# Splitting fp32 weights with two GpSimd transfers instead of ScalarE and VectorE

## The chip, the cores and the metric

The kernel runs on one core of a Trainium2 chip, as one program of some 18,000 instructions. The metric is the device time of one execution in microseconds. A core has TensorE (PE in the profile; PEld is its weight load), VectorE (DVE), ScalarE (ACT), GpSimd (POOL) and SyncE (SP). Each engine works through its own queue in order; semaphores tie them together. DMAs are issued by SyncE, ScalarE or GpSimd and carried by 16 DMA engines.

## The reference

Two transformer blocks in fp32 on x of 512 x 1024 (d_model 1024, one batch, depth 1):

```python
def first_block(x, ...):
    x = x + 0.5 * swiglu_ffn(rmsnorm(x, ffn1_norm), ffn1_w_gate, ffn1_w_up, ffn1_w_down)   # d_ff 2816
    x = x + hybrid_mixer(rmsnorm(x, mix_norm), w_in, ..., w_out)   # 8 heads of chunked attention + pooling
    x = x + 0.5 * swiglu_ffn(rmsnorm(x, ffn2_norm), ffn2_w_gate, ffn2_w_up, ffn2_w_down)
    return rmsnorm(x, final_norm)

def second_block(x, ...):
    proj = rmsnorm(x, norm_mix_pre) @ w_in
    ...                                   # 4 heads of differential attention, 4 heads of mLSTM
    x = x + rmsnorm(concat(o_diff, o_mlstm) @ w_out, norm_mix_post)
    u = square(relu(rmsnorm(x, norm_mlp_pre) @ w_up))              # d_ff 4096
    return x + rmsnorm(u @ w_down, norm_mlp_post)
```

All weight matrices are fp32, 136 MB together, and each is used once.

## The kernel before, in words

Every product of activations and weights is made of three TensorE products of rounded numbers. An fp32 operand is split into a rounded part (type fp32r) and a remainder (also fp32r); hi x hi, hi x lo and lo x hi are added up in one PSUM bank (`mm3`). The activations' parts are xh and xl (or tiles of the arenas, which the profile calls a1f, a1r, a2f, a2r: f holds fp32, r holds fp32r). The weights' parts are whi and wlo.

The weights are cut into 256 tiles of 128 x 1024 numbers or a little less, listed by `plan` in the order in which TensorE needs them. Most are 8 blocks of 128 rows x 128 columns, so that each partition gets 8 rows of 512 bytes; some (the values' projections, the last MLP's down projection) are 2 blocks x 512 columns, with rows of 2 KB. One tile feeds 24 matmuls of 512 columns. A tile goes through three steps: SyncE loads it into one of three raw buffers (wraw), ScalarE copies it with rounding into one of four whi buffers, and VectorE subtracts whi from wraw into one of four wlo buffers (`split`, called from `w_pump`). `W` hands TensorE's code the tile that is due and lets `w_pump` run two tiles ahead of it; at four places the code asks for four tiles at once.

The code is only noted down at first. Each call becomes an `Op` with its reads, writes and an assumed duration, and `issue` sets the order of each engine's queue by repeated forward and backward sweeps over the graph of dependencies. It runs twice, once for the first block's feed-forward part and mixer (arena a1), once for the rest (a2). A DMA that GpSimd issues is booked there as 1000 ns of GpSimd, one that SyncE issues as 60 ns, and all transfers share one modelled bus. So the order of all queues changes with every edit.

The stages, in time: first feed-forward block (to 377 us), first mixer with attention and pooling (to 560), second feed-forward block (to 925), second block's attention and mLSTM (to about 1195), last MLP. The last MLP's up projections take the 128-column tiles, its down projections the 512-column ones.

Of the kernel before, what the change touches and what calls it, by code (L numbers as in the profile page):

```python
# [9 lines left out]
F32 = mybir.dt.float32  # L10
F32R = mybir.dt.float32r
I32 = mybir.dt.int32
AF = mybir.ActivationFunctionType
ALU = mybir.AluOpType

P = 128
# [4 lines left out]
KD = 8  # L21
EPS = 1e-6
NEG = -1e30
W_BUFS = 4
R_BUFS = 3
SPLIT_AHEAD = 2
ARENA = (5500, 16050)
ARENA2 = (10450, 11050)

# [35 lines left out]
class Program:  # L65
# [84 lines left out]
    def note(self, eng, fn, a, k):  # L150
        outs = list(a[:1]) + [k[n] for n in ("out", "accum_out") if k.get(n) is not None]
        ins = [x for x in a[1:] if self.is_ap(x)]
        ins += [x for n, x in k.items() if n not in ("out", "accum_out") and self.is_ap(x)]
        op = self.add(eng.name, getattr(eng.queue, fn), a, k, self.cost(eng.name, fn, outs, ins, k))
        if "dma" in fn:
            op.dma = max(math.prod(outs[0].shape) / 90.0, 300.0)
            op.lag = 1900.0 + op.dma
        w, r = self.boxes(outs), self.boxes(ins)
        op.opens = eng.name == "PE" and k.get("start", True)
        if fn == "matmul" and not op.opens:  # L160
            r = r + w
        if k.get("func") in (AF.Ln, AF.Exp, AF.Silu, AF.Tanh):
            self.edge(self.load, op)
            self.users.append(op)
        for bs, wr in ((r, False), (w, True)):
            for b in bs:
                for c in self.cells(b):
                    for b2, o2, w2 in self.seen.get(c, ()):
                        if o2 is not op and (wr or w2 or c[0].startswith('bank')) and self.meet(b, b2, op, o2):
                            self.edge(o2, op, w2 and not wr)  # L170
        for b in w:
            for c in self.cells(b):
                self.seen[c] = [x for x in self.seen.get(c, ()) if not self.covers(b, x[0])]
        for bs, wr in ((r, False), (w, True)):
            for b in bs:
                for c in self.cells(b):
                    self.seen.setdefault(c, []).append((b, op, wr))
# [137 lines left out]
class Kern:  # L315
# [114 lines left out]

    def w_init(self, pool):
        self.L = self.plan()
        self.raw = [pool.tile([P, 1024], F32, name=f"wraw{i}") for i in range(R_BUFS)]
        self.wh = [pool.tile([P, 1024], F32R, name=f"whi{i}") for i in range(W_BUFS)]
        self.wl = [pool.tile([P, 1024], F32R, name=f"wlo{i}") for i in range(W_BUFS)]
        self.w_dma = self.w_split = self.w_cur = 0

    def w_view(self, t, i):
        _, _, nk, nc_ = self.L[i]
        return t[:, :nk * nc_].rearrange("p (k c) -> p k c", k=nk)  # L440

    def w_load(self, upto):
        while self.w_dma < min(upto, len(self.L)):
            i = self.w_dma
            self.sp.dma_start(self.w_view(self.raw[i % R_BUFS], i), self.L[i][1])
            self.w_dma += 1

    def w_pump(self, upto):
        while self.w_split < min(upto + 1, len(self.L)):
            i = self.w_split  # L450
            self.w_load(i + R_BUFS)
            m = self.L[i][2] * self.L[i][3]
            step = m // 2 if i < 2 else m
            for c in range(0, m, step):
                c = slice(c, c + step)
                self.split(self.wh[i % W_BUFS][:, c], self.wl[i % W_BUFS][:, c], self.raw[i % R_BUFS][:, c])
            self.w_split += 1
            self.w_load(self.w_split + R_BUFS)

    def W(self, key, ahead=SPLIT_AHEAD):  # L460
        i = self.w_cur
        assert self.L[i][0] == key, (self.L[i][0], key)
        self.w_pump(i + ahead)
        self.w_cur += 1
        return self.w_view(self.wh[i % W_BUFS], i), self.w_view(self.wl[i % W_BUFS], i)

# [83 lines left out]
    def setup(self):  # L550
        tc, I, ctx = self.tc, self.I, self.ctx
        cp = ctx.enter_context(tc.tile_pool(name="cp", bufs=1))
        pp = ctx.enter_context(tc.tile_pool(name="pp", bufs=1, space=bass.MemoryType.PSUM))
        self.B = [pp.tile([P, 512], F32, name=f"bank{i}") for i in range(8)]
        self.mmb = Rot(self.B)
        dp = ctx.enter_context(tc.tile_pool(name="dp", bufs=1, space=bass.MemoryType.DRAM))
        self.tape = dp.tile([8, 16, 384], F32, name="tape")

        T = lambda name, shape, dt=F32: cp.tile(shape, dt, name=name)
        self.w_init(cp)  # L560
        self.X, self.XT = T("X", [P, KD, S]), T("XT", [P, NT, D])
        self.xh, self.xl = T("xh", [P, KD, S], F32R), T("xl", [P, KD, S], F32R)
        self.xs = [(self.xh[:, m, :], self.xl[:, m, :]) for m in range(KD)]
        self.ident, self.onesr = T("ident", [P, P]), T("onesr", [P, P], F32R)
        self.hm2 = T("hm2", [P, 2])
        self.rows1, self.rows, self.cols = T("rows1", [8, P]), T("rows", [NROW, P]), T("cols", [P, 8 + NROW])
        self.rcol = T("rcol", [P, NT])
        self.cv, self.ct, self.cr = (T(n, [P, 16]) for n in ("cv", "ct", "cr"))
        self.gfp = T("gfp", [P, KD])
        self.rsb, self.acc = T("rsb", [P, S]), T("acc", [P, S])  # L570
        self.sqh, self.sql = T("sqh", [P, S], F32R), T("sql", [P, S], F32R)
        self.sq = Rot([T(f"sq{i}", [P, S]) for i in range(2)])

        def load_x(m):
            self.sp.dma_start(self.XT[:, :, m * P:(m + 1) * P],
                              I["x"][0][:, m * P:(m + 1) * P].rearrange("(t p) c -> p t c", p=P))
        self.ac.dma_start(self.rows1, I["ffn1_norm"][0].rearrange("(r c) -> r c", c=P))
        self.po.memset(self.ident, 1.0)
        for s in (1, -1):
            self.po.affine_select(out=self.ident, in_=self.ident, pattern=[[s, P]], base=0, channel_multiplier=-s,  # L580
                                  compare_op=ALU.is_ge, fill=0.0)
        for half in range(2):
            for m in range(4 * half, 4 * half + 4):
                load_x(m)
                if m == 4 * half:
                    for i in range(2):
                        k = slice(m, m + 4)
                        self.sp.dma_start(self.w_view(self.raw[i], i)[:, k, :], self.L[i][1][:, k, :])
        self.w_dma = 2
        self.w_load(R_BUFS)  # L590
        self.prog.table(LN_EXP)
        self.act(self.onesr, self.ident, AF.Copy, scale=0.0, bias=1.0)
        self.ci = {"g1": 0}
        r = 0
        for name, src, n in [
            ("gm", I["mix_norm"][0], 8), ("g2", I["ffn2_norm"][0], 8),
            ("gf", I["final_norm"][0], 8), ("gp", I["norm_mix_pre_2"][0], 8), ("gu", I["norm_mlp_pre_2"][0], 8),
            ("psc", I["pool_scale"][0], 4), ("cb", I["conv_b_2"][0], 4), ("dn", I["diff_norm_2"][0], 1),
        ]:
            self.po.dma_start(self.rows[r:r + n, :], src.rearrange("(r c) -> r c", c=P))  # L600
            self.ci[name] = 8 + r
            r += n
        self.po.dma_start(self.rows[r:r + 16, :], I["conv_w_2"][0].rearrange("j (r c) -> (j r) c", c=P))
        self.ci["cw"] = 8 + r
        r += 16
        self.po.dma_start(self.rows[r:r + 4, :], I["mlstm_norm_2"][0])
        self.ci["ln"] = 8 + r
        r += 4
        for nm, key in (("qn", "q_norm"), ("kn", "k_norm")):
            for d in range(2):  # L610
                self.po.dma_start(self.rows[r:r + 1, d * 64:(d + 1) * 64], I[key])
            self.ci[nm] = 8 + r
            r += 1
        assert r == NROW
        self.po.dma_start(self.hm2, I["k_hm2"])
# [500 lines left out]
    def mlstm_phase(self):  # L1116
        I = self.I
        with self.mem.scope() as T:
            mv = T([P, NT, 4, P + 1])
# [14 lines left out]
            self.ve.memset(mv[:, :, :, P:P + 1], 1.0)  # L1134

            self.mmb = Rot(self.B[0:2])
            ww = [self.W(("mv", kk), 3 - kk) for kk in range(4)]
            for t in range(NT):
                b = self.bank()
                self.tgroup(b, ww, self.xs, t)  # L1140
# [1 line left out]
                         scale=self.rcol[:, t:t + 1])  # L1142
# [75 lines left out]
    def mlp_phase(self):  # L1218
        I = self.I
        X, y = self.X, self.y  # L1220
        with self.mem.scope() as T:
# [17 lines left out]
            self.ve.tensor_copy(gcol, b[:, :8])  # L1239


            ww = [self.W(("o2B", i), 3 - i) for i in range(4)]
            for a in range(2):
                cols = slice(a * H2, (a + 1) * H2)
                acc = self.acc[:, cols]
# [43 lines left out]
            for c in range(4):  # L1289
# [15 lines left out]
                for half in range(2):  # L1305
                    hs = slice(half * S, (half + 1) * S)
                    if c < 3 or half == 0:
                        banks = [self.bank() for _ in range(NT)]
                        self.tgroup_k(banks, [("md", c, half, kk) for kk in range(4)], us)
                        for t in range(NT):  # L1310
# [3 lines left out]
                                self.tt(y[:, t, hs], banks[t], y[:, t, hs], ALU.add)  # L1314
                            else:
                                post(t, hs, banks[t], 0)
            ww = [self.W(("md", 3, 1, kk), 3 - kk) for kk in range(4)]
            for t in range(NT):
                cuts = [(S, S)] if t < NT - 1 else [(S, H2), (S + H2, H2)]
                for i, (c0, n) in enumerate(cuts):  # L1320
# [18 lines left out]
                step = S if t < NT - 1 else H2  # L1339
# [70 lines left out]
```

## Time and profile before

| | us |
|---|---|
| median of 2 runs | 1547.52 (1547.42 to 1547.62) |
| profiled execution | 1547.03 |
| its span, first to last instruction | 1545.2 |
| TensorE busy in the span | 1525.7 |
| VectorE busy | 824.6 |
| ScalarE busy | 648.4 |
| GpSimd busy | 297.7 |

The profile is of one execution. The span is what its views cut up; 1.8 us lie around it. An engine's busy time doesn't count the issuing of DMAs. A matmul counts as busy from its start to a modelled end, and the next one overlaps it, so that a busy TensorE can still be delayed.

### The profile page before, as it was taken

How to read it: one execution, taken by the hardware profiler on the slowest of the kernel's cores; microseconds unless marked ns; L12 is line 12 of the kernel's file. 1: busy time of each engine (PE TensorE's matmuls, PEld its weight loads, DVE VectorE, ACT ScalarE, POOL GpSimd, SP SyncE). 2: the span in 40 equal slices, each digit the busy share in tenths (PEclk: the TensorE clock that was granted, in tenths of full speed). 3: DMA queues.
4: the chain of work that ended last, by engine and by line, in shares of the span. 5: the costliest groups of instructions: out<-in, count | busy, mean ns of one | idle time of the engine just before them, and what ended most of it. 6: DMA issues, size and time to landing. Idle time of an engine off the chain costs nothing.

```text
span 1545.2 us, 18001 instructions
## 1 busy us (share of the span) xinstructions
PE 1525.7 (99%) x6931; PEld 1235.2 (80%) x6931; DVE 824.6 (53%) x1284; ACT 648.4 (42%) x1063; POOL 297.7 (19%) x290
## 2 busy tenths in 40 slices
PE   9999999999999999999999999999999999999997
PEld 7888888788877788888888887677788888888886
DVE  6443443336588884433443467998568524344345
ACT  6322232234367663312322275776555634233232
POOL 5120120212243321101200146331016000000002
PEclk9999999999999999999999999999999999999999
DMA  6333333533311133333433233121221332333321
GB/s 192 96 99 95 96 103 96 114 94 111 96 55 41 55 110 96 95 96 96 113 96 95 79 99 102 42 82 49 90 69 45 123 93 95 96 95 97 95 95 55
DMA packets 226757, 140.68 MB, mean 91 GB/s; under 512 B 5340, under 2 KB 212800, under 8 KB 226672
## 3 DMA queue, kind: packets, MB, share of 16 engines
q1 hardware_dynamic: 224832, 136.33, 30.1%
q0 software_dynamic: 1824, 3.21, 1.0%
q8 instruction: 54, 0.88, 0.2%
q14 instruction: 31, 0.25, 0.1%
q10 hardware_dynamic: 16, 0.00, 0.0%
HBM read 137.23 MB, written 2.29 MB: 90 GB/s over the span
## 4 chain that ended last, share of the span: by engine, by line
PE 92%; DVE 6%; ACT 1%; POOL 0%; issue 0%; DMA 0%; SPq 0%; DVEq 0%; POOLq 0%; ACTq 0%
PE bank L232 92%; DVE a2f L232 1%; DVE wlo L232 1%; ACT a2f L232 1%; DVE X L232 1%; DVE a2r L232 0%; DVE XT L232 0%; DVE xl L232 0%; DVE a1r L232 0%; DVE sq L232 0%; DMA XT<-x 0%; DVE cv L232 0%; POOL a2f L232 0%; DVE acc L232 0%; POOL acc L232 0%
## 5 line engine op out<-in xcount | busy, mean ns | idle before, releaser
L232 DVE TENSOR_TENSOR wlo<-wraw,whi 128x1024 fp32r<-128x1024 f32 (+2 forms) x258 | 325.2, 1262 | 417.8 <-ACT whi L232 352.9
L232 ACT ACTIVATE whi<-wraw 128x1024 fp32r<-128x1024 f32 (+2 forms) x258 | 267.5, 1039 | 518.8 <-PE bank L232 498.5
L232 PE MATMUL bank<-xl,whi 128*128 128x512 f32 (+1 forms) x1272 | 463.5, 384 | 2.5 <-DVE xl L232 2.5
L232 PE MATMUL bank<-xh,whi 128*128 128x512 f32 (+1 forms) x1272 | 462.6, 385 | 1.8 <-DVE a1r L232 1.0
L232 PE MATMUL bank<-xh,wlo 128*128 128x512 f32 (+1 forms) x1272 | 458.2, 383 | 0.0
L232 PEld LDWEIGHTS bank<-xl,whi 128*128 128x128 f32 x1272 | 239.4, 189 | 50.0 <-DVE xl L232 2.9
L232 PEld LDWEIGHTS bank<-xh,whi 128*128 128x128 f32 x1272 | 238.9, 189 | 49.7 <-issue 2.2
L232 PEld LDWEIGHTS bank<-xh,wlo 128*128 128x128 f32 x1272 | 239.1, 189 | 46.5 <-issue 1.9
L232 PE MATMUL bank<-whi,a2r 128*128 128x512 f32 (+1 forms) x528 | 155.6, 388 | 0.0
L232 PE MATMUL bank<-a1r,whi 128*128 128x512 f32 x480 | 151.2, 400 | 0.0
L232 PE MATMUL bank<-a2r,whi 128*128 128x512 f32 x416 | 130.0, 397 | 0.0
L232 POOL TENSOR_TENSOR a1f<-a1f 128x512 f32<-128x512 f32 x40 | 59.5, 1487 | 317.1 <-DVE a1f L232 311.6
L232 PEld LDWEIGHTS bank<-whi,a2r 128*128 128x128 f32 x528 | 98.2, 188 | 21.0
L232 POOL TENSOR_TENSOR a2f<-a2f 128x512 f32<-128x512 f32 x38 | 56.4, 1484 | 303.5 <-DVE a2f L232 252.3
L232 PEld LDWEIGHTS bank<-a1r,whi 128*128 128x128 f32 x480 | 89.7, 188 | 22.1 <-issue 0.9
L232 PE MATMUL bank<-wlo,a2r 128*128 128x512 f32 (+1 forms) x264 | 95.0, 389 | 0.0
L232 PEld LDWEIGHTS bank<-a2r,whi 128*128 128x128 f32 x416 | 77.3, 187 | 19.0 <-issue 0.7
L232 PE MATMUL bank<-a1r,wlo 128*128 128x512 f32 x240 | 91.1, 399 | 0.0
L232 ACT ACTIVATE a2r<-a2f 128x512 fp32r<-128x512 f32 (+3 forms) x83 | 51.0, 620 | 93.3 <-POOL a2f L232 55.3
L232 DVE TENSOR_TENSOR a2r<-a2f,a2r 128x512 fp32r<-128x512 f32 (+2 forms) x81 | 54.8, 680 | 49.7 <-ACT a2r L232 48.9
L232 PE MATMUL bank<-a2r,wlo 128*128 128x512 f32 x208 | 79.4, 397 | 0.0
L232 POOL TENSOR_TENSOR X<-X,a2f 128x512 f32<-128x512 f32 (+1 forms) x9 | 10.7, 1210 | 337.6 <-ACT a2f L232 337.6
(246 smaller groups left out, 1586.0 us busy)
## 6 DMA issues: line engine op xcount, KB each, us to landing
wraw<-ffn_w_gate SPq DMA_DIRECT2D x43, 512.0 KB, 3.8
wraw<-ffn_w_up SPq DMA_DIRECT2D x43, 512.0 KB, 3.8
wraw<-w_in SPq DMA_DIRECT2D x40, 512.0 KB, 3.9
wraw<-ffn_w_down SPq DMA_DIRECT2D x32, 512.0 KB, 3.9
wraw<-w_up SPq DMA_DIRECT2D x32, 512.0 KB, 4.0
wraw<-w_down SPq DMA_DIRECT2D x32, 512.0 KB, 3.6
wraw<-w_out SPq DMA_DIRECT2D x16, 512.0 KB, 3.5
wraw<-ffn_w_down SPq DMA_DIRECT2D x16, 384.0 KB, 3.4
```

Of the source, the lines that this page charges most:

```text
L232: op.fn(*op.a, **op.k)
```

## The change

The raw buffers go. For each tile GpSimd issues a DMA from the fp32 weights into a whi tile of type fp32r, which rounds on the way; ScalarE then writes -whi into wlo; then GpSimd issues a second DMA from the same weights that adds them to wlo. The weights are therefore read twice. There are five whi and five wlo buffers in place of four, and `W` runs three tiles ahead in place of two. The first two tiles are made in halves, as before. The planner is told that an accumulating DMA also reads its destination.

```diff
-W_BUFS = 4
-R_BUFS = 3
-SPLIT_AHEAD = 2
+W_BUFS = 5
+SPLIT_AHEAD = 3
...
-        if fn == "matmul" and not op.opens:
+        if (fn == "matmul" and not op.opens) or k.get("accum_op") is not None:
             r = r + w
...
-    def w_load(self, upto):
-        while self.w_dma < min(upto, len(self.L)):
-            i = self.w_dma
-            self.sp.dma_start(self.w_view(self.raw[i % R_BUFS], i), self.L[i][1])
-            self.w_dma += 1
-
     def w_pump(self, upto):
-        while self.w_split < min(upto + 1, len(self.L)):
-            i = self.w_split
-            self.w_load(i + R_BUFS)
-            m = self.L[i][2] * self.L[i][3]
-            step = m // 2 if i < 2 else m
-            for c in range(0, m, step):
-                c = slice(c, c + step)
-                self.split(self.wh[i % W_BUFS][:, c], self.wl[i % W_BUFS][:, c], self.raw[i % R_BUFS][:, c])
-            self.w_split += 1
-            self.w_load(self.w_split + R_BUFS)
+
+
+        while self.w_made < min(upto + 1, len(self.L)):
+            i = self.w_made
+            h, l = self.wh[i % W_BUFS], self.wl[i % W_BUFS]
+            src, m, nk = self.L[i][1], self.L[i][2] * self.L[i][3], self.L[i][2]
+            n = 2 if i < 2 else 1
+            vh, vl = self.w_view(h, i), self.w_view(l, i)
+            for q in range(n):
+                k, c = slice(q * nk // n, (q + 1) * nk // n), slice(q * m // n, (q + 1) * m // n)
+                self.po.dma_start(vh[:, k, :], src[:, k, :])
+                self.act(l[:, c], h[:, c].bitcast(F32), AF.Copy, scale=-1.0)
+                self.po.dma_start(vl[:, k, :], src[:, k, :], accum_op=ALU.add)
+            self.w_made += 1
...
-                if m == 4 * half:
-                    for i in range(2):
-                        k = slice(m, m + 4)
-                        self.sp.dma_start(self.w_view(self.raw[i], i)[:, k, :], self.L[i][1][:, k, :])
-        self.w_dma = 2
-        self.w_load(R_BUFS)
```

GpSimd's queue shows the move best. At the end of the first third of the first feed-forward block it held, before, almost only the products of up and gate (a1f) and a few small loads; a row ending in x6 stands for six in a row:

```order
L232 DMA hm_89<-k_hm 128x2
L232 TENSOR_TENSOR a1f<-a1f 128x512 x6
L232 DMA a1f<-k_anti 128x128
L232 DMA a1f<-rel_bias 8x257
L232 MEMSET a1f 8x128
L232 TENSOR_TENSOR a1f<-a1f 128x512
```

In the changed kernel the same products stand between pairs of weight transfers (whi_72 to whi_76 and wlo_77 to wlo_81 are the five buffers each; a load into whi waits for TensorE to be done with the buffer, one into wlo for ScalarE's negation):

```order
L231 DMA wlo_79<-ffn_w_gate 128x8x128
L231 DMA whi_76<-ffn_w_gate 128x8x128
L231 DMA wlo_80<-ffn_w_up 128x8x128
L231 TENSOR_TENSOR a1f<-a1f 128x512
L231 DMA whi_72<-ffn_w_up 128x8x128
L231 DMA wlo_81<-ffn_w_gate 128x8x128
L231 TENSOR_TENSOR a1f<-a1f 128x512
L231 DMA wlo_77<-ffn_w_up 128x8x128
L231 DMA whi_73<-ffn_w_down 128x8x128
L231 TENSOR_TENSOR a1f<-a1f 128x512
```

whi_72 goes with wlo_77, and so on to whi_76 with wlo_81. So the second load of a tile (wlo_80) stands behind the first load of the next tile (whi_76), and the products come between them.

In the second block's attention, GpSimd scales the exponentials of a softmax (TENSOR_SCALAR, four widths for one head) and makes products for the rotary embedding. Before:

```order
L232 TENSOR_TENSOR a2f<-a2f 128x512 x6
L232 TENSOR_SCALAR a2f<-a2f 128x384
L232 TENSOR_SCALAR a2f<-a2f 128x256
L232 TENSOR_SCALAR a2f<-a2f 128x512
L232 TENSOR_TENSOR a2f<-a2f 128x512
L232 TENSOR_SCALAR a2f<-a2f 128x128
```

Now, at the same place, transfers of the next projections' weights stand ahead of the scalings and between them:

```order
L231 TENSOR_TENSOR a2f<-a2f 128x512 x2
L231 DMA whi_74<-w_in 128x8x128
L231 DMA wlo_77<-w_in 128x8x128
L231 TENSOR_SCALAR a2f<-a2f 128x512
L231 TENSOR_SCALAR a2f<-a2f 128x384
L231 TENSOR_SCALAR a2f<-a2f 128x256
L231 TENSOR_TENSOR a2f<-a2f 128x512 x2
L231 TENSOR_SCALAR a2f<-a2f 128x128
L231 DMA wlo_79<-w_in 128x8x128
L231 DMA whi_75<-w_in 128x8x128
```

At the start, GpSimd made the identity matrix for the transposes of x (ident), before, and then only small loads, while SyncE loaded raw halves between the loads of x:

```order
L232 MEMSET ident 128x128
L232 ISA
L232 AFFINE_SELECT ident<-ident 128x128 x2
L232 DMA rows<-mix_norm 8x128
L232 DMA rows<-ffn_norm 8x128
```

Now the first weights' transfers stand around it (128x4x128 is half a tile):

```order
L231 DMA whi_72<-ffn_w_gate 128x4x128
L231 MEMSET ident 128x128
L231 ISA
L231 AFFINE_SELECT ident<-ident 128x128
L231 DMA whi_72<-ffn_w_gate 128x4x128
L231 AFFINE_SELECT ident<-ident 128x128
L231 DMA whi_73<-ffn_w_up 128x4x128
L231 DMA whi_75<-ffn_w_up 128x8x128
L231 DMA wlo_77<-ffn_w_gate 128x4x128
```

The first load into wlo comes after four loads into whi, and the identity is ready two issues later than before.

## Rows read from the trace of the kernel before

**Rows 1.** Page, parts 1 and 4: engine totals, and the chain that ended last.

```profile
PE 1525.7 (99%) x6931; PEld 1235.2 (80%) x6931; DVE 824.6 (53%) x1284; ACT 648.4 (42%) x1063; POOL 297.7 (19%) x290
...
PE 92%; DVE 6%; ACT 1%; POOL 0%; issue 0%; DMA 0%; SPq 0%; DVEq 0%; POOLq 0%; ACTq 0%
PE bank L232 92%; DVE a2f L232 1%; DVE wlo L232 1%; ACT a2f L232 1%; DVE X L232 1%; DVE a2r L232 0%; DVE XT L232 0%; DVE xl L232 0%; DVE a1r L232 0%; DVE sq L232 0%; DMA XT<-x 0%; DVE cv L232 0%; POOL a2f L232 0%; DVE acc L232 0%; POOL acc L232 0%
```

**Rows 2.** TensorE's waits: for whom, us in total, times, longest us.

```profile
PE bank L232 <- DVE xl L232: 2.5, 2, 2.2
...
PE bank L232 <- ACT xh L232: 0.8, 1, 0.8
```

**Rows 3.** Busy time by stretch; first row names the columns.

```profile
core 0: us, PE busy (x) PEld busy (x) DVE busy (x) ACT busy (x) POOL busy (x), PEclk, DMA share, GB/s
50.00:90.00 40.00, 40.00 (x178) 33.14 (x177) 16.62 (x18) 12.38 (x15) 5.30 (x7) 1.00 0.32 94
100.00:150.00 50.00, 50.00 (x216) 40.32 (x216) 17.57 (x20) 10.02 (x10) 2.22 (x1) 1.00 0.34 101
...
430.00:560.00 130.00, 128.72 (x582) 96.59 (x582) 110.60 (x226) 88.56 (x175) 47.91 (x53) 1.00 0.20 61
950.00:1130.00 180.00, 177.71 (x825) 132.77 (x824) 141.08 (x338) 123.47 (x277) 49.00 (x52) 1.00 0.24 69
1130.00:1200.00 70.00, 66.67 (x453) 61.14 (x453) 52.95 (x118) 35.99 (x82) 27.04 (x34) 0.95 0.20 56
```

**Rows 4.** Groups by form: split on VectorE and ScalarE, products on GpSimd.

```profile
L232 DVE TENSOR_TENSOR wlo<-wraw,whi 128x1024 fp32r<-128x1024 f32 x238 | 306.3, 1288 | 398.9 <-ACT whi L232 339.6 <-PE bank L232 51.3 <-ACT a1r L232 7.8
...
L232 ACT ACTIVATE whi<-wraw 128x1024 fp32r<-128x1024 f32 x238 | 251.6, 1059 | 507.5 <-PE bank L232 491.6 <-issue 6.6 <-DVE X L232 5.2
...
L232 POOL TENSOR_TENSOR a1f<-a1f 128x512 f32<-128x512 f32 x40 | 59.5, 1487 | 317.1 <-DVE a1f L232 311.6 <-ACT a1f L232 5.1
```

**Rows 5.** Instructions on wlo alone by stretch; the last count is VectorE's subtractions.

```profile
430.00:560.00 130.00, 47.46 (x118) 22.24 (x119) 18.02 (x14) 1.00 0.20 61
950.00:1130.00 180.00, 67.23 (x172) 32.05 (x171) 27.71 (x23) 1.00 0.24 69
1130.00:1200.00 70.00, 37.26 (x132) 24.97 (x132) 11.46 (x9) 0.95 0.20 56
```

**Rows 6.** Tiles' views: time of issues, ns min/median/max; us to landing.

```profile
L232 POOL DMA_DIRECT2D a2f<-w_in x1: 976/976/976, 754.4 to 754.4; - x1
...
L232 POOL DMA_DIRECT2D a1f<-pool_w x1: 838/838/838, 194.2 to 194.2; - x1
...
L232 POOL DMA_DIRECT2D a2f<-k_rope x1: 579/579/579, 742.2 to 742.2; - x1
...
L232 SPq DMA_DIRECT2D wraw<-ffn_w_gate x45: 367/368/1107, 2.4 to 850.7; - x45
...
L232 POOL DMA_DIRECT2D XT<-tape x8: 530/532/553, 299.1 to 306.2; - x8
...
DMA to landing us min/median/max: 3.3/6.7/8.3
```

**Rows 7.** DMA issues: count, KB each, median us to landing.

```profile
a2f<-k_rope POOLq DMA_DIRECT2D x1, 512.0 KB, 5.2
```

**Rows 8.** DMA queues, 50 to 90 us: packets, MB, share of 16 engines.

```profile
q1 hardware_dynamic: 7252, 3.66, 31.0%
```

**Rows 9.** Timeline at the start: start us, duration us, engine, operation.

```profile
7.60 0.63 ACT L232 ACTIVATE whi<-wraw 128x512 fp32r<-128x512 f32 x1 [1.02 <-DMA wraw<-ffn_w_gate]
...
8.26 0.69 DVE L232 TENSOR_TENSOR wlo<-wraw,whi 128x512 fp32r<-128x512 f32 x1 [0.49 <-ACT whi L232]
...
9.39 0.78 PE L232 MATMUL bank<-xh,whi 128*128 128x512 f32 x1
...
11.09 0.62 PE L232 MATMUL bank<-xh,wlo 128*128 128x512 f32 x1
```

More of the change, by code (lines that the diff above doesn't have):

```diff
@@ L432, in w_init @@
         self.L = self.plan()
-        self.raw = [pool.tile([P, 1024], F32, name=f"wraw{i}") for i in range(R_BUFS)]
         self.wh = [pool.tile([P, 1024], F32R, name=f"whi{i}") for i in range(W_BUFS)]
         self.wl = [pool.tile([P, 1024], F32R, name=f"wlo{i}") for i in range(W_BUFS)]
-        self.w_dma = self.w_split = self.w_cur = 0
+        self.w_made = self.w_cur = 0
     def w_view(self, t, i):
@@ L462, in W @@
         assert self.L[i][0] == key, (self.L[i][0], key)
-        self.w_pump(i + ahead)
+        self.w_pump(max(i + ahead, i))
         self.w_cur += 1
@@ L1136, in mlstm_phase @@
             self.mmb = Rot(self.B[0:2])
-            ww = [self.W(("mv", kk), 3 - kk) for kk in range(4)]
+            ww = [self.W(("mv", kk), 4 - kk) for kk in range(4)]
             for t in range(NT):
@@ L1239, in mlp_phase @@
             self.ve.tensor_copy(gcol, b[:, :8])
-            ww = [self.W(("o2B", i), 3 - i) for i in range(4)]
+            ww = [self.W(("o2B", i), 4 - i) for i in range(4)]
             for a in range(2):
@@ L1316, in mlp_phase @@
                                 post(t, hs, banks[t], 0)
-            ww = [self.W(("md", 3, 1, kk), 3 - kk) for kk in range(4)]
+            ww = [self.W(("md", 3, 1, kk), 4 - kk) for kk in range(4)]
             for t in range(NT):
```

## Prediction

> **What bounds the kernel now.** I read the page first: engine totals and the chain that ended last [rows 1]. TensorE is busy 1525.7 of 1545.2 us and holds 92% of the chain; VectorE is the only other engine with a share worth naming (6%), the subtraction that makes the remainders has 1%. TensorE's own waits say the same from the other side: the longest of the seven groups that the view lists is 2.5 us in two pieces, the shortest 0.8 us [rows 2]. Then I cut the span into stages [rows 3]. In the dense stages (the two feed-forward blocks, and the last MLP's up projections) TensorE is busy all of every stretch, at the full granted clock of 1.00, 178 matmuls in 40 us: 225 ns each, so 24 x 225 = 5.4 us for one weight tile. VectorE is at 0.4 there, the DMA engines at 0.32 to 0.34. In the attention stages (430 to 560, 950 to 1130 us) TensorE still counts as busy 99%, but VectorE is busy 110.6 of 130 and 141.1 of 180 us: there it is the second limit. The only places where TensorE is visibly short of work are the start, the end and 1130 to 1200 us (66.7 of 70 us, clock 0.95 on average). So all that a change beside TensorE can gain is the 19.5 us between busy and span, plus what is hidden in stretched matmuls of the attention stages; 2% of this kernel is 31 us. I take 2% as about what a measurement here can tell from no change.
>
> **The split that goes.** 258 subtractions leave VectorE, 238 of them of 1288 ns and 306.3 us; the chain holds 1% of the span of them. The rounding copies on ScalarE (238 of 1059 ns) are replaced one for one by copies of the same size with a factor of -1: nothing saved, nothing added [rows 4]. The first attention stretch has 14 of them and the second 23 [rows 5]: 14 x 1.29 = 18 and 23 x 1.29 = 30 us, so VectorE falls from 0.85 to 0.71 and from 0.78 to 0.62. What is late next is TensorE itself, busy 99% of both stages. I take -5 us; the bounds are 0 and -14, the 1.3, 2.3 and 3.3 us of idle TensorE in the three stretches [rows 3] and as much again for stretched matmuls.
>
> **The two transfers, issue.** Instead of one load on SyncE's queue (368 ns of that queue [rows 6]) each of the 256 tiles now takes two issues by GpSimd. Nearest rows: a load of GpSimd with the same number of rows (128 x 8, each shorter) took 976 ns of the engine, one of 128 x 4 rows of the same length 838, one of 128 long rows 579 [rows 6]. The accumulating issue may take more, since it has a second thing to read: 1.0 to 1.5 us, I take 1.0. So 2.0 us of GpSimd in 5.4 us of TensorE, beside one multiplication of 1487 ns [rows 4] every two tiles: (4.0 + 1.5) of 10.8 us, half busy. In the dense stages this hides.
>
> **The two transfers, latency.** A tile's chain is now issue 1.0, landing about 5.2 (the longest 512 KB load that GpSimd issues [rows 7]), negation 1.06, issue 1.0, landing again: 13 to 15 us if the addition lands like a plain load, 20 if it takes twice as long. With five buffers a slot comes free four tiles before its next use, 4 x 5.4 = 21.6 us. The order shows that each first load stands one tile ahead of the second one of the tile before, so it isn't held up by it. Hidden, with 2 to 8 us in hand; if that cover went, each tile would pay the difference.
>
> **The two transfers, DMA time.** Here it is decided. The present loads alone make the 0.32 to 0.34 share of the dense stages (0.31 of the 0.32 are their queue's own) [rows 3, 8]. The first new transfer moves the same bytes in the same pieces: 0.32 again. The rounding inside it can't be faster than the plain load and no row shows one that costs more; I take the same. The second has no row. Its lower bound is a plain load, 0.32; then the sum is 0.64. It must read its destination besides its source: two row times, 0.64, sum 0.96. If reading, reading and writing can't overlap at all it is three, 0.96, sum 1.28. Farther off stands the slowest load that GpSimd issues now: eight of 128 KB, issued from 299.1 to 306.2 us and 6.7 us to landing at the median [rows 6], so 1 MB in about 13 us, 7 us for 512 KB; that would be a sum of 1.6. I take two row times, 0.96, because the plain row is the nearest and the destination's read is the one thing that is certainly added. That is below 1 in the stages with 0.32 and a hair above it in the down projections (0.34 x 3 = 1.02), which are some 30% of 890 dense us: 0.02 x 270 = +5 us. The wide tiles of the last MLP's down projections and of the values have rows four times as long and are less dense: no loss.
>
> The Trainium skill, "Collectives: The Full Stack", section "Part 3: Why 7× under link rate", says that an addition made by the DMA engines costs no cycles of its own but two source reads in the same ring, and shows the rate falling from 62.28 to 32.35 GB/s. By that rule the second transfer would be two row times and the sum 0.96, as taken; no run before shows an accumulating transfer, so it is untested here.
>
> **Start.** In the present kernel the first matmul with rounded weights starts at 9.39 us and the first with the remainder at 11.09; the remainder's first half is ready at 8.95, 1.35 us after the rounding began [rows 9]. In the new order GpSimd issues four first loads ahead of the first second load, which lands about 5 us after the negation: 7.6 (as now) + 0.6 + 0.8 + 4 to 5 = 13 to 14 us. TensorE can fill a part with the products that need no remainder, and the order does so. Then x, five first loads and as many second ones compete. +6 us; bounds +2 and +15.
>
> **GpSimd's queue in the attention stages.** GpSimd is busy 47.9 of 130, 49.0 of 180 and 27.0 of 70 us there [rows 3]. The tiles are 14, 23 and 9, 46 together [rows 5]; at 2.0 us each they bring it to 0.58, 0.53 and 0.64. Each issue can also wait for TensorE (a slot) or ScalarE (a negation), and the softmax scalings and products queue behind it; the order shows two issues ahead of the scalings of a softmax. 53 + 52 + 34 = 139 GpSimd operations stand in these stretches; if one in four meets an issue, loses half of it, and half of the losses matter, that is 139 x 0.25 x 0.5 x 0.5 = 9 us. I take +8; bounds 0 and the 46 x 2 x 1.0 = 92 us of all issues.
>
> **Sum.** The profiled execution took 1547.0 us, half a microsecond under the median, with 1.8 us around its span. 1547 - 5 + 5 + 6 + 8 = **1561 us**, +0.9%.
>
> **Rivals.** *A, the forecast:* the DMA engines keep up, 1540 to 1578 us by the bounds above. For it: the share is known and three times it fits; five buffers. Against it: it fits by 4%. *B, the DMA engines become the bound* (slower): if the second transfer costs more than 2.1 plain loads, weights arrive slower than TensorE uses them, and five buffers hold back only 27 us once. At three row times the dense stages stretch by 1.28: 0.28 x 890 = +249 us, 1561 - 5 + 249 = **1805 us**; at the far row's 1.6, some 2090. For it: no row shows such a transfer and the margin is thin. Against it: nothing in the trace says that reads and writes of different rows can't overlap; plain loads show they do. *C, GpSimd's queue becomes the second limit* (slower): half of the 92 us lands on the chain in place of the 8, 1553 + 46 = **1599 us**. For it: in-order waits for slots ahead of softmax work. Against it: GpSimd waits for VectorE much of these stages anyway, and VectorE is what gets relief. *D, issues held up by VectorE* (slower): each issue lasts longer by one VectorE operation, 0.69 us [rows 9]. In the dense stages that hides; in attention it is 92 x 0.69 = 63 us, half of it on the chain: 1561 + 32 = **1593 us**. Against it: the present issues take 0.5 to 1.0 us [rows 6] and show no such wait. *E, the relief is worth more:* VectorE's chain in the attention stages shrinks and neither queue nor start costs anything: 1547 - 14 = **1533 us**; 2% isn't in reach, since 19.5 us is all the idle time there is.
>
> The Trainium skill, "SBUF — State Buffer", section "SBUF: two separate sides", has D as a trap: descriptors that GpSimd writes must wait while VectorE runs an operation in a two-port mode. No row before shows it at work.
>
> **How the numbers follow.** A 0.46, B 0.36 (a third of it under 1700, a third above 1850), C 0.10, D 0.03, E 0.05. Likeliest is A: 1561, its own range 1540 to 1578. Over 2% faster would need more than E: 0.02. Slower by over 2% are B, C and D: 0.49; within 2% are A and most of E: 0.49. The range from 1536 to 1850 leaves out the far end of E and the upper third of B, with the far row.
>
> **What the new profile would show.** Right: DMA share near 0.9 in the dense stages with TensorE at 1.00 busy and 225 ns a matmul; GpSimd issues near 1.0 us; VectorE at 0.6 to 0.7 in attention; start later by about 6 us. B: TensorE waiting for the landing of a second load at every tile, DMA share at its ceiling, and perhaps a clock below 1.00 after the waits. C: dense stages unchanged, attention stages longer, ScalarE and VectorE waiting for GpSimd. Wrong altogether if the rounding transfer itself is slower than a plain load, or an issue takes several microseconds of GpSimd, either of which no row here excludes.

## The result, and the profile after

| | before | after |
|---|---|---|
| median, us | 1547.52 | 1729.66 (1727.60 to 1731.73) |
| profiled execution, us | 1547.03 | 1727.60 |
| its span, us | 1545.2 | 1725.9 |
| mean granted clock of TensorE | 0.996 | 0.965 |

The change makes the kernel slower: 1.118 times the time before, 95% interval 1.112 to 1.123. The time lies inside the range of the prediction, but not where its likeliest case had put it (1561, at most 1578).

The page of the changed kernel, its parts 1, 3 and 4: engine totals, the queue of GpSimd's transfers (packets, MB, share of 16 engines), and the chain that ended last.

```profile
PE 1581.9 (92%) x6931; PEld 1257.8 (73%) x6931; DVE 530.9 (31%) x1026; ACT 638.5 (37%) x1063; POOL 862.2 (50%) x806
...
q0 software_dynamic: 440160, 267.48, 101.5%
...
issue 32%; PE 21%; POOL 20%; DMA 16%; DVE 6%; ACT 4%; SPq 0%; POOLq 0%; ACTq 0%; DVEq 0%
PE bank L231 21%; POOL whi L231 8%; POOL wlo L231 8%; DMA whi<-ffn_w_up 3%; DMA whi<-ffn_w_gate 3%; DMA whi<-ffn_w_down 3%; ACT wlo L231 2%; POOL a2f L231 2%; POOL a1f L231 2%; DMA whi<-w_in 2%; DMA whi<-w_down 1%; DVE a2f L231 1%; DMA wlo<-ffn_w_gate 1%; DVE xl L231 1%; DMA wlo<-w_up 1%
```

Against [rows 1], TensorE holds 21% of the chain in place of 92%. Its place is taken by the path of a weight: GpSimd's issues of whi and wlo, the transfers of both, ScalarE's wlo (the negation). The largest part, 32%, is "issue": time in which an engine waited for nothing that the profile shows. VectorE is down from 824.6 to 530.9 us, as forecast, and it bought nothing that can be seen here.

Where is the loss? I noted in the traces when the n-th matmul with a whi or wlo operand started (6240 in all, 24 to most tiles). The dense stretch from the 300th to the 1500th, 50 tiles' worth, took 276.8 us before and 315.7 after: 5.54 and **6.31 us a tile**. By stage, cut where the order of `plan` ends one, how far the changed kernel, and three of the experiments below, fall behind the kernel before, in us:

| stage (matmuls with weights) | before took | after | e2 | e5 | e8 |
|---|---|---|---|---|---|
| start (to the 300th) | 80.8 | +15.5 | +7.4 | +11.9 | +7.4 |
| first feed-forward block (to 1584) | 296.4 | +45.0 | +0.4 | 0.0 | 0.0 |
| first mixer (to 2160) | 183.3 | +9.8 | -1.9 | +0.4 | -2.1 |
| second feed-forward block (to 3744) | 363.2 | +56.3 | +1.6 | +3.4 | 0.0 |
| second block's attention (to 4608) | 249.9 | +13.8 | +7.5 | +17.5 | +15.2 |
| last MLP | 362.3 | +39.2 | -2.6 | +1.0 | +0.3 |

140 of the 180 us are lost in the three dense stages, which the prediction had as hidden but for 5 us. The first mixer loses 9.8, all of it up to the 1968th matmul, where it is 10.5 behind. The windows of the dense stages after (columns as in [rows 3], whose first two rows they answer to):

```profile
core 0: us, PE busy (x) PEld busy (x) DVE busy (x) ACT busy (x) POOL busy (x), PEclk, DMA share, GB/s
50.00:90.00 40.00, 39.60 (x174) 32.19 (x173) 7.52 (x11) 11.18 (x14) 24.94 (x27) 1.00 1.17 175
100.00:150.00 50.00, 44.46 (x181) 35.19 (x180) 8.18 (x13) 10.13 (x12) 25.65 (x23) 0.93 1.09 156
300.00:340.00 40.00, 39.16 (x171) 30.56 (x170) 4.09 (x9) 8.24 (x9) 16.77 (x13) 1.00 1.38 189
```

216 matmuls in 50 us have become 181, some of them at a lower clock. A share above 1 looks like DMA engines that are the bound. But the traffic of 100 to 140 us, cut into 40 slices of 1 us, has holes:

```profile
DMA  2999991100008999999994399999969999992009
GB/s 26 141 181 188 299 204 13 15 0 0 0 0 96 170 178 222 309 323 291 312 217 53 47 156 182 172 181 174 146 80 176 179 231 350 248 262 54 0 2 113
```

From 106 to 112 us the DMA engines move next to nothing. A resource that is the bound doesn't rest. Who keeps them waiting is in the chain of waits after (engine and tile, for whom; us in total, times, longest):

```profile
POOL wlo L231 <- ACT wlo L231: 595.7, 170, 8.5
...
ACT wlo L231 <- DMA whi<-ffn_w_down: 196.1, 38, 10.8
...
ACT wlo L231 <- DMA whi<-ffn_w_up: 142.6, 34, 10.8
...
POOL whi L231 <- PE bank L231: 106.2, 52, 7.6
```

GpSimd stands 595.7 us before second loads, waiting for ScalarE's negation; the negation waits for the landing of the first load. Only 106.2 us does GpSimd wait for TensorE to give up a buffer, which is what it should wait for if it ran ahead. GpSimd's timeline from 764 us shows what stands behind such a wait (start us, duration us, operation, idle time before it and who ended it):

```profile
764.60 1.56 POOL L231 DMA_DIRECT2D wlo<-ffn_w_down  x1 [6.10 <-ACT wlo L231]
768.82 1.57 POOL L231 DMA_DIRECT2D wlo<-ffn_w_gate  x1 [2.66 <-ACT wlo L231]
769.71 1.58 POOL L231 DMA_DIRECT2D whi<-ffn_w_up  x1
770.69 1.49 POOL L231 DMA_DIRECT2D whi<-ffn_w_gate  x1
778.91 1.57 POOL L231 DMA_DIRECT2D wlo<-ffn_w_up  x1 [6.73 <-ACT wlo L231]
779.82 1.56 POOL L231 DMA_DIRECT2D whi<-ffn_w_up  x1
780.81 2.15 POOL L231 DMA_DIRECT2D wlo<-ffn_w_gate  x1
781.71 2.14 POOL L231 DMA_DIRECT2D whi<-ffn_w_gate  x1
789.45 1.57 POOL L231 DMA_DIRECT2D wlo<-ffn_w_up  x1 [5.59 <-ACT wlo L231]
790.35 1.57 POOL L231 DMA_DIRECT2D whi<-ffn_w_up  x1
793.85 1.56 POOL L231 DMA_DIRECT2D wlo<-ffn_w_gate  x1 [1.93 <-ACT wlo L231]
800.23 1.55 POOL L231 DMA_DIRECT2D wlo<-ffn_w_up  x1 [4.83 <-ACT wlo L231]
```

Take the load at 769.71 into whi. Its negation starts at 777.56, after ScalarE had waited 9.04 us for this transfer:

```profile
777.56 1.06 ACT L231 ACTIVATE wlo<-whi 128x1024 fp32r<-128x1024 f32 x1 [9.04 <-DMA whi<-ffn_w_up]
```

The second load follows at 778.91. Only then, with no idle time of their own, come the first load at 779.82 and the pair behind it: they waited for nothing but their turn. Six second loads in 35.6 us are 5.9 us a tile, where TensorE takes 5.54.

How many tiles share one such round trip is set by the order of the queue. I counted, in the order in which the trace has GpSimd's issues, how many first loads of later tiles stand ahead of each of the 258 second loads (the **lead**): none for 69, one for 170, two or more for 19. A round trip is landing 7.7 + negation 1.06 + 0.3 to the issue + 0.9 to the next issue = 10.0 us. With a lead of none that is 10.0 us for a tile, with one 5.0, with two 3.3: 6.2 us on average over the 258. As an estimate that is close to the measured 6.31, and above the 5.54 that TensorE takes. The closeness is partly luck, because a second load without a lead costs less than a whole round trip where its first load went out before the pause, as the one at 770.69 did. A replay of GpSimd's queue in the trace's order (0.9 us from issue to issue, each second load at least 1.36 us behind the landing of its first) gives 5.4 us over the same 50 tiles with 7.7 us for every landing. With each load's own landing (up to 11.5 us) and GpSimd's products in between it gives 6.1: the late landings and the products in that queue belong to the pace.

TensorE then waits, for the landing of second loads above all (the first two groups of its list):

```profile
PE bank L231 <- DMA wlo<-ffn_w_up: 25.6, 16, 5.0
PE bank L231 <- DMA wlo<-ffn_w_down: 20.7, 12, 3.1
```

A wait can cost more than itself. TensorE from 116 to 136 us (us, busy and count, granted clock, DMA share, GB/s):

```profile
116.00:120.00 4.00, 3.72 (x16) 1.00 1.93 309
120.00:124.00 4.00, 1.24 (x5) 1.00 1.03 118
124.00:128.00 4.00, 1.55 (x4) 0.62 1.41 177
128.00:132.00 4.00, 4.00 (x11) 0.53 1.16 146
132.00:136.00 4.00, 4.00 (x19) 1.00 1.68 273
```

TensorE was busy 2.8 of the 8 us to 128; within them the granted clock falls to half, the 1.2 GHz level, and then 11 matmuls are done in the time of 19, until the full 2.4 GHz is back. Over the span the mean clock fell from 0.996 to 0.965. By that 0.031 x 1726 = 54 us is about the most that the clock itself can have cost of the 180: part of it fell into time in which TensorE had no weights anyway, and no run takes the two apart.

### The profile page after: what moved, and what is told of

Its sections match the earlier page's. It is cut to its first block, busy times and chain, and to the rows that moved or that the text cites. A ratio compares the mean times of both kernels' runs of the same rounds, so it can differ in the third digit from the quotient of the medians.

```text
span 1725.9 us, 18311 instructions
## 1 busy us (share of the span) xinstructions
PE 1581.9 (92%) x6931; PEld 1257.8 (73%) x6931; DVE 530.9 (31%) x1026; ACT 638.5 (37%) x1063; POOL 862.2 (50%) x806
## 4 chain that ended last, share of the span: by engine, by line
issue 32%; PE 21%; POOL 20%; DMA 16%; DVE 6%; ACT 4%; SPq 0%; POOLq 0%; ACTq 0%; DVEq 0%
PE bank L231 21%; POOL whi L231 8%; POOL wlo L231 8%; DMA whi<-ffn_w_up 3%; DMA whi<-ffn_w_gate 3%; DMA whi<-ffn_w_down 3%; ACT wlo L231 2%; POOL a2f L231 2%; POOL a1f L231 2%; DMA whi<-w_in 2%; DMA whi<-w_down 1%; DVE a2f L231 1%; DMA wlo<-ffn_w_gate 1%; DVE xl L231 1%; DMA wlo<-w_up 1%
## 5 line engine op out<-in xcount | busy, mean ns | idle before, releaser
L231 ACT ACTIVATE wlo<-whi 128x1024 fp32r<-128x1024 f32 (+2 forms) x258 | 267.4, 1038 | 776.0 <-DMA whi<-ffn_w_down 196.1
L231 PE MATMUL bank<-xh,wlo 128*128 128x512 f32 (+1 forms) x1272 | 472.7, 391 | 51.8 <-DMA wlo<-ffn_w_up 25.6
L231 PE MATMUL bank<-xh,whi 128*128 128x512 f32 (+1 forms) x1272 | 470.2, 391 | 4.7 <-ACT xh L231 3.4
L231 POOL DMA_DIRECT2D wlo<-ffn_w_down x48 | 77.6, 1624 | 138.7 <-ACT wlo L231 138.0
L231 PE MATMUL bank<-a2r,whi 128*128 128x512 f32 x416 | 136.9, 417 | 7.6 <-ACT a2r L231 7.3
L231 POOL DMA_DIRECT2D wlo<-ffn_w_up x45 | 72.9, 1620 | 137.4 <-ACT wlo L231 132.0
L231 DVE TENSOR_TENSOR a2r<-a2f,a2r 128x512 fp32r<-128x512 f32 (+3 forms) x81 | 55.6, 690 | 228.6 <-ACT a2r L231 227.7
L231 POOL DMA_DIRECT2D wlo<-ffn_w_gate x45 | 75.2, 1670 | 82.7 <-ACT wlo L231 77.2
L231 POOL DMA_DIRECT2D wlo<-w_up x32 | 52.5, 1667 | 108.5 <-ACT wlo L231 86.6
L231 POOL DMA_DIRECT2D wlo<-w_down x32 | 39.6, 1237 | 111.6 <-ACT wlo L231 111.3
L231 PE MATMUL bank<-a2r,wlo 128*128 128x512 f32 x208 | 82.8, 416 | 11.5 <-DMA wlo<-ffn_w_down 11.5
```

The source lines that it names most:

```text
L231: op.fn(*op.a, **op.k)
```

## The experiments

Two theories first. **T**, the prediction's rival B: the DMA engines' time is the bound. **L**: the chain of a tile (first landing, negation, second landing) in GpSimd's in-order queue, with five buffers, is; the DMA engines have holes because of it. When T had fallen, I split L: **Q**, the order in that queue is what hurts, and it comes from the planner's short times for GpSimd's transfers; **B**, in these expectations, the chain is too long for five buffers whatever the order (not the prediction's B). Kernels run once were compared with runs of the kernel before on the same chip (medians 1547.3 to 1547.8, single runs 1546.8 to 1550.1), so a few us between two of them say nothing.

**e1, e2: which of the two.**

```diff
 e1
-                self.po.dma_start(vl[:, k, :], src[:, k, :], accum_op=ALU.add)
+                self.po.dma_start(vl[:, k, :], src[:, k, :])
 e2
-                self.act(l[:, c], h[:, c].bitcast(F32), AF.Copy, scale=-1.0)
+                if i < W_BUFS:
+                    self.act(l[:, c], h[:, c].bitcast(F32), AF.Copy, scale=-1.0)
```

> The second transfer copies the weights over wlo instead of adding them, so wlo is left as the rounded weights and not the remainder; all waits and the queue's order stay. Theory T (the DMA engines' time is the bound: a 512-byte row took 42 ns in the first transfer and 65 ns in the second, 107 ns x 64 rows = 6.8 us per tile against 5.4 of TensorE): both transfers cost 42, 84 ns x 64 = 5.4 us, so the time falls to 1550 to 1600 us. Theory L (the chain load, negation, load through GpSimd's in-order queue and five buffers sets the pace, with gaps in the DMA engines): only the second landing gets shorter, by 1 to 2 us of some 24, so 1650 to 1700 us.

> ScalarE's negation is left out from the sixth tile on, so the second transfer adds to what the buffer held and waits for the buffer alone, not for the first transfer. Bytes, kinds and number of transfers stay. Theory T: nothing changes in the DMA engines, 1700 to 1740 us. Theory L: the two transfers of a tile run side by side, the chain is some 9 us shorter, 1550 to 1600 us, and GpSimd's waits for ScalarE's wlo (595.7 us) are gone.

e1 took 1573.03 us, e2 1560.03. e1 lies in T's range (1550 to 1600) and misses L's (1650 to 1700), so by itself it spoke for T. e2 decides: it has all transfers of the change, with the additions, and only the wait for ScalarE is gone (the planner sets the order anew with it, as with most edits). T had 1700 to 1740 for it, so T falls. Its windows, and what GpSimd's loads wait for:

```profile
50.00:90.00 40.00, 40.00 (x178) 33.14 (x177) 7.61 (x11) 4.95 (x8) 28.31 (x30) 1.00 1.40 208
300.00:340.00 40.00, 40.00 (x178) 33.12 (x177) 7.61 (x11) 4.51 (x8) 26.41 (x28) 1.00 1.62 215
```

```profile
POOL whi L231 <- PE bank L231: 416.6, 157, 8.3
...
POOL wlo L231 <- PE bank L231: 124.1, 54, 6.4
```

178 matmuls in 40 us, as before, at a DMA share of 1.62: higher than where the changed kernel lost time. These loads now wait only for buffers. In e1 the order of GpSimd's queue is the very same as in the changed kernel (69 second loads without a lead), but the first loads land sooner, which L's forecast had not reckoned with; the view of whi, after and then e1:

```profile
DMA to landing us min/median/max: 3.9/7.7/11.5
```

```profile
DMA to landing us min/median/max: 3.9/5.0/11.3
```

The round trip is then 5.0 + 2.3 = 7.3 us, by the same estimate 4.5 us a tile (by the full replay 4.8), below 5.54; the dense stretch measured 5.54. So the bad order does no harm in the dense stretch where first loads land in 5.0 us, and slow landings do none if nobody waits for them (e2's whi: 6.1 at the median, wlo 7.8): in these runs the loss needed both. e1 doesn't change the first landing alone: second loads land in 5.0 us too, in place of 6.8.

**e3, e4: fewer and more buffers.**

```diff
 e3 (and 3 - kk, 3 - i for 4 - kk, 4 - i at the three places that ask for four tiles)
-W_BUFS = 5
-SPLIT_AHEAD = 3
+W_BUFS = 4
+SPLIT_AHEAD = 2
 e4 (and H_BUFS in place of W_BUFS where wh is indexed)
+H_BUFS = 6
-        self.wh = [pool.tile([P, 1024], F32R, name=f"whi{i}") for i in range(W_BUFS)]
+        self.wh = [pool.tile([P, 1024], F32R, name=f"whi{i}") for i in range(H_BUFS)]
```

> Four buffers each and two tiles ahead, as in the kernel before. Theory T: a bound by transfer time hardly cares, 1730 to 1760 us. Theory L: the same chain is spread over four tiles, the dense stages' period grows from 6.1 towards 6.1 x 5/4 = 7.7 us, 1900 to 2000 us.

> Six whi buffers and five wlo buffers (the room of one tile that the change freed). Theory T: 1715 to 1735 us. Theory L: first transfers may start a tile earlier, up to 5.4 us of the chain is hidden, 1600 to 1680 us.

e3 took 1769.84 us, e4 1607.01. e3 fits neither theory: 10 us past T's range, far under L's. Without the fifth pair of buffers the kernel is only 40 us slower. e4 fits L, but not for the reason that I had given. The number of buffers also changed the order: in e4 second loads without a lead are 5 in place of 69, in e3 they are 79. GpSimd's wait in e4:

```profile
POOL wlo L232 <- ACT wlo L232: 337.3, 175, 5.5
```

So the number of buffers isn't tested by itself here, and the next step was to change the order alone.

**e5: the order alone.** The planner is told that a GpSimd transfer lands later: for a whole tile 5.4 us after its issue (first) and 6.4 (adding), in place of 3.4. These are its formula's figures; the medians in the changed kernel are 7.7 and 6.8. Program, buffers and transfers stay.

```diff
+            if eng.name == "POOL":
+                op.dma = math.prod(outs[0].shape) / (45.0 if k.get("accum_op") is not None else 70.0)
+                op.lag = 3500.0 + op.dma
```

> Only the planner's assumed durations of GpSimd's DMAs change, towards what the trace shows (landing some 5.4 us after the issue for a first transfer and 6.4 for an adding one, and their share of the bus); five buffers, same instructions, another order. Theory Q (in GpSimd's in-order queue a second transfer that waits for the negation holds up the first transfers behind it, because the planner thought that it would not wait): 1560 to 1640 us, GpSimd's wait for ScalarE's wlo (595.7 us) at least halved. Theory B (the chain is simply too long for five buffers, whatever the order): 1700 to 1740 us.

1583.65 us, so Q. Second loads without a lead: 13; with two or more: 62. GpSimd's two longest waits:

```profile
POOL whi L234 <- PE bank L234: 328.2, 160, 8.2
...
POOL wlo L234 <- ACT wlo L234: 241.2, 135, 5.6
```

The two groups have changed places: GpSimd is ahead and mostly waits for buffers to come free. The dense stretch is back at 5.54 us a tile. 146 of the 182 us come back by the order alone. The planner reorders the other queues too; but the replay of GpSimd's queue, which takes nothing of them but the landings, gives 4.4 us a tile for e5's order and landings (6.2 at the median) and 6.1 for the changed kernel's. That points at this queue.

**e6, e7, e9, e10: each new transfer by itself.** In e6 GpSimd rounds with its load, but SyncE loads raw too and VectorE subtracts. In e7, e9 and e10 SyncE loads raw, ScalarE rounds and negates, GpSimd adds; e7 has one raw buffer and five pairs, e9 three and four pairs, as the kernel before has, and e10 is e9 with the planner's times of e5.

```diff
 e6 (three raw buffers, four pairs)
-                self.act(l[:, c], h[:, c].bitcast(F32), AF.Copy, scale=-1.0)
-                self.po.dma_start(vl[:, k, :], src[:, k, :], accum_op=ALU.add)
+                self.sp.dma_start(self.w_view(r, i)[:, k, :], src[:, k, :])
+                self.tt(l[:, c], r[:, c], h[:, c].bitcast(F32), ALU.subtract)
 e7, e9, e10
-                self.po.dma_start(vh[:, k, :], src[:, k, :])
+                self.sp.dma_start(self.w_view(r, i)[:, k, :], src[:, k, :])
+                self.act(h[:, c], r[:, c], AF.Copy)
```

> The rounding transfer alone: GpSimd loads whi with rounding, SyncE loads the raw weights into three raw buffers, VectorE subtracts; four buffers each and two tiles ahead, as before the change. No instruction waits in GpSimd's queue for another engine's work on the same tile. Theory Q: harmless but for the start, 1550 to 1570 us. Theory B: the chain is one landing and a subtraction, 1550 to 1570 us. If the rounding transfer itself were the trouble: over 1600 us.

> The adding transfer alone: SyncE loads one raw buffer, ScalarE rounds it into whi and negates whi into wlo, GpSimd adds the weights to wlo; five buffers each. GpSimd's queue has one transfer per tile, and no first transfer stands behind it. Theory Q: 1550 to 1590 us. Theory B: load and rounding (5 us) still stand in the chain with negation, issue and landing (9.5 us), but the raw load runs ahead, 1550 to 1620 us. If the adding transfer were too slow in itself: over 1650 us.

> The adding transfer alone, as in e7, but with the buffers of the kernel before (three raw, four whi, four wlo), so that the raw buffer is no longer a limit of its own: SyncE loads raw, ScalarE rounds and then negates, GpSimd adds. There is no first transfer in GpSimd's queue, so a waiting second one holds up only the products. If the convoy of first loads behind waiting second loads is the cause: 1550 to 1610 us. If an adding transfer of GpSimd behind a wait is a loss by itself (four buffers too few, the products behind it late): 1640 us or more, with TensorE waiting for the landing of wlo in the dense stages.

> The kernel of e9 with the planner told that a transfer of GpSimd lags by 3.5 us and its bytes, as in e5. Order alone differs from e9. If the planner's short times are what costs time: 20 us or more under e9 and under 1610. If the chain behind one adding transfer is too long for four buffers: within 15 us of e9.

e6 took 1575.64 us, e7 1652.04, e9 1588.91, e10 1575.62. e6 is 6 us past what I expected, with losses at the start (+9.4), in the first mixer (+6.3) and in the second block's attention (+9.1); its dense stretch is 5.55 us a tile. e7 missed both theories, and by its number it fell into the third case, an adding transfer too slow in itself. But two of its waits tell of a limit that I had built in:

```profile
POOL wlo L231 <- ACT wlo L231: 758.0, 204, 10.9
...
ACT whi L231 <- DMA wraw<-ffn_w_up: 127.0, 40, 6.2
```

A single raw buffer is reloaded only when ScalarE is done with it, so SyncE's load can't run ahead. With three raw buffers (e9, with four pairs in place of five) the dense stretch is 5.63 us a tile in place of 6.02, though GpSimd stands before wlo for longer than in the changed kernel (595.7 us):

```profile
POOL wlo L231 <- ACT wlo L231: 670.4, 184, 14.5
ACT whi L231 <- PE bank L231: 424.9, 180, 10.0
```

That is the point of e9: **in the dense stretch the same wait costs next to nothing (5.63 against 5.54 us a tile) where no first load stands behind it.** Its 41 us behind the kernel before lie elsewhere, the start (+12.3) and the last MLP (+12.9) first. The planner's times matter little there: e10 is 13 us less, by its numbers the second case, though e9 had shown already that four buffers do for one adding transfer. There is one transfer per tile to place, and nothing behind it that a round trip depends on.

**e8: everything mended.** Six whi buffers, the planner's times of e5, and the first three tiles loaded by SyncE and split by ScalarE and VectorE as before.

```diff
+                if i < 3:
+                    r = self.mem.whole[F32][:, 2304 + 1024 * i:3328 + 1024 * i]
+                    self.sp.dma_start(self.w_view(r, i)[:, k, :], src[:, k, :])
+                    self.split(h[:, c], l[:, c], r[:, c])
+                    continue
```

> Six whi buffers, the planner's durations as in the run with them, and the first three tiles loaded by SyncE into idle scratch and split by ScalarE and VectorE as before the change. All loss in the dense stages should go (Q and B alike), and of the start's 7 to 15 us all but 2: 1545 to 1560 us. If VectorE's relief in the attention stages is worth anything, under 1545.

1568.26 us (four runs, 1564.30 to 1569.88), 1.0125 times the kernel before (95% interval 1.0104 to 1.0146): past my 1560, and still behind. The dense stages are even, the first mixer is 2.1 us ahead. What stays is the start (+7.4) and the second block's attention (+15.2). No kernel of this study beats the one before.

## Why the prediction was right or wrong, by its steps

The range held the time by luck, because it was wide enough for B; the likeliest case, A, was wrong, and so were the mechanism of B and the place of C. (A's upper end, 1578, doesn't follow from "the bounds above" either, one of which is +92.)

- **The two transfers, latency: this step failed.** "Hidden, with 2 to 8 us in hand" was reckoned for one buffer: a slot comes free 21.6 us before its next use. The chain of waits runs through GpSimd's queue instead. "Each first load stands one tile ahead ..., so it isn't held up by it" was read from one place in the order, and it drew the wrong conclusion there too: the first load of the tile after next stands behind the second load, which waits for a landing. At 69 of 258 places there is no lead at all. The landing was low as well: 5.2 us taken, 7.7 measured for whi, 6.8 for wlo. With 5.2 the same estimate gives 4.6 us a tile. Either error alone would have done little harm in the dense stages: e1 (order as it was, landing 5.0) and e5 (other order, landing 6.2) are within 4 us of the kernel before in each of them.
- **The two transfers, DMA time: forecast 0.96 and a ceiling at 1.** The share was 1.1 to 1.6 and no ceiling (e2). The rounding transfer costs more than a plain one, which the prediction had excluded from its sum but named at its end; the adding one costs 2.4 plain ones. Rival B stood on "more than 2.1 plain loads"; that came true, and its consequence did not. Two of B's signs came as well, TensorE waiting for second landings and a lower clock, but the queue's mechanism gives the same signs; the ceiling, its third, did not come. B's time, 1805, is near the measured one by accident.
- **Issue: 1.0 us.** An issue is recorded with some 1.55 us, but successive ones start 0.9 to 1.0 us apart (778.91, 779.82, 780.81, 781.71 above). The term holds as a pace.
- **Start: +6, bounds 2 to 15.** The 300th matmul came 15.5 us late, 7.4 us in e2 and e8. x is later too: the loads of x land 7.2 us after their issue at the median and 11.0 at most (e8: 8.5 and 11.5), before 5.6 and 6.2. Since e8 is as late as e2 with its first tiles loaded the old way, I put its 7.4 us on that, by these landings alone; no run took the other early transfers away.
- **GpSimd's queue in the attention stages: +8.** The second block's attention lost 13.8 us in the changed kernel. With no wait for ScalarE it is +7.5 (e2), with the mended order +15.2 (e8): issues alone are about the forecast term, issues that wait about twice that. That the queue is the cause here is argued from these sums; no run took the loads out of this stage alone. Rival C named the right mechanism, a queue worked in order, and the wrong place.
- **VectorE's relief: -5.** The first mixer is 1.9 and 2.1 us ahead in e2 and e8, one profile each, and nothing more is to be seen. VectorE was busy less, but TensorE had been busy 99% there ([rows 3]).
- **D, issues held up by VectorE.** The Trainium skill, "SBUF — State Buffer", section "SBUF: two separate sides", makes GpSimd's descriptor writing wait while VectorE runs an operation in a two-port mode. In e1, whi's issues have medians of 0.71 to 0.88 us by tensor, with VectorE busy a third of the span; no run here shows the trap.
- **Addition by the DMA engines.** By the rule of the Trainium skill, "Collectives: The Full Stack", section "Part 3: Why 7× under link rate" (no cycles of its own, two source reads in one ring), it would cost two plain loads. Measured in the last section: 2.4, near the rule but above it.

## What to carry to other kernels

When a tile's path goes twice through the same in-order queue with a wait between, count the round trip of that queue, not that of the buffer alone. As a rough guide, its time (issue, landing, the other engine's step, issue) divided by one more than the number of later first loads that stand ahead of the second must stay well under the time in which a tile is used up, since late landings and other work in the queue come on top. Count those leads over the whole order before trusting one place, and give the planner that sets the order a landing near the measured one. And look for holes in the DMA engines' traffic before a share near 1 is called the bound.

## What the runs showed of the hardware

**DMA packets that round or add take longer, and overlap.** A packet here is one row of 512 bytes of a transfer. The queues from 50 to 90 us (packets, MB, share), in e6 (q0 rounds, q1 loads plainly) and in e9 (q0 adds):

```profile
q0 software_dynamic: 7324, 3.68, 56.5%
q1 hardware_dynamic: 8110, 4.09, 36.1%
```

```profile
q0 software_dynamic: 8159, 4.11, 82.7%
q1 hardware_dynamic: 7505, 3.79, 33.7%
```

Share x 640 us of engine time, divided by packets of some 500 bytes: 49 ns for rounding, 65 ns for adding, 28 and 29 ns for plain loads beside them ([rows 8]: 27 ns). That is 1.8 and 2.4 plain loads. (The medians of the 512-byte packets alone are 42, 65 and 27 ns.) It isn't GpSimd's queue that makes them slow: in the kernel before, 16 plain packets of 2 KB in it (190 to 205 us) took 84 ns at the median, as SyncE's of 2 KB did over the span. Both together would fill 1.3 of the DMA engines, and did (1.40 in e2), with TensorE never short: packets on one engine must overlap in time, and this share isn't bounded by 1.

**The landing of a rounding load varies with what runs beside it.** The same loads into whi, 512 KB each and in the same order of issue (though not at the same times), landed in 5.0 us at the median when the second transfer was a rounding one too (e1), and in 7.7 us beside adding ones in the changed kernel. With other orders it was 6.1 to 7.2 us beside adding ones (e2 to e5, e8), and 5.2 us beside plain loads (e6), so the kind of the neighbours isn't all of it. The record of a rounding issue depends on what stands ahead of it: 0.93 us at the median where an adding one had started more than 1.3 us earlier, 1.55 us where less (changed kernel, 70 and 113 issues); in e1 it is 0.87 and 0.88 behind a second rounding one.
